# A hybrid decoder layer on one core: where the second norm's scale and shift are applied, which engine runs the first conv taps and the chain scalings, and when g2 is summed

## The chip, the cores and the metric

The kernel runs on one core of one Trainium2 chip. The metric is device time in microseconds (us); smaller is better. In the views of the profile PE is TensorE, DVE is VectorE, ACT is ScalarE, POOL is GpSimd and SP is SyncE, which issues nearly all DMAs here. PE multiplies; DVE, ACT and POOL do elementwise work; PE's results land in PSUM, from where DVE or ACT take them.

## The reference

One layer, sequence 1024, model width 1024, float32. The second half is what the change is mostly about: the norm before the MLP is `rms_norm(x, norm_mlp_w) * (1 + sc2) + sh2`.

```python
mod = silu(c) @ w_mod + b_mod                       # six vectors of 1024
sh1, sc1, g1, sh2, sc2, g2 = split(mod, 6)
h = rms_norm(x, norm_mix_w) * (1 + sc1) + sh1
proj = h @ w_in                                     # lx, ly, q, k, v, z, beta, alpha
xr = conv4(x_lru) + lru_conv_b                      # causal, 4 taps, per channel
out_lru = rms_norm(rg_lru(xr, gates) * gelu(y_lru), lru_norm_w)
q, k, v = split(silu(conv4(qkv)))                   # 4 heads of 128
out_gdn = rms_norm(gated_delta_rule(q, k, v, g, beta)) * silu(z)
x = x + g1 * (concat(out_lru, out_gdn) @ w_out)
h = rms_norm(x, norm_mlp_w) * (1 + sc2) + sh2
x = x + g2 * (square(relu(h @ w_up)) @ w_down)
return rms_norm(x, final_norm_w)
```

The gated delta rule is computed in chunks, one after the other for each head: `v_new = u - w @ state`, then the output and the next state from `v_new`.

## The kernel before

All of it is recorded first, operation by operation, and then put in order by a planner inside the kernel (`Recorder.schedule`). The large matmuls of PE are a "backbone" that keeps its written order. Everything else is placed by a list scheduler that knows a cost for each operation, a due time (how long before the backbone needs it), a bias that makes an operation less urgent (`rec.bias`), and how many buffers are free: 43 tiles of 128x1024 (`big`), later 6 more, and 8 PSUM banks. The planner's result is a fixed order for every engine; on the chip each engine runs its own list in order and waits where an operand is late. Every instruction is emitted from one line, L329, so the profile's rows are told apart by tile names and not by lines.

Almost every product is done in three matmuls: each float32 operand is split into a high part (an ACT copy to a shorter float, suffix `h`) and a low part (the remainder, a subtraction on DVE or POOL, suffix `l`), and high x high, high x low and low x high are added in PSUM (`mm3`). So each operand costs one ACT and one DVE or POOL instruction before PE can use it.

In order of time the stages are:

- **Start** (to about 65 us): x is loaded, the first modulation vectors are summed from `w_mod`, x is transposed.
- **Keys and gates** (to about 186 us): projections k0 to k3 and z0 to z3; in parallel the 64x64 triangular blocks are inverted.
- **Chains** (to about 420 us): for heads 0 to 3 the projections q and v, and `chain(h)`, 8 steps in a row. A step is: PE `ch<-S` (not in the first), DVE `r = nv - ch`, PE `ch<-r,LT`, a scaling of that PSUM piece of 128x128 by a column (`vn`, line 1018), PE `ch<-vn,ktl`, DVE `S` (the next state). The steps run between projection matmuls, which keep PE busy meanwhile.
- **LRU** (to 465 us): projections lx0..lx3 and ly0..ly3, and `lru(ct)`: a four-tap conv (`conv`, lines 813 to 819; tile `xr`), split of `xr`, gate matmuls, tanh, exp and sqrt on ACT (`ta`, `ti`, `aa`, `a`), a scan on DVE, a gelu (`tg`, `ly_st`), a store.
- **wg** (from 465 us) and **wl** (from 530 us, to 580): the output projection. wg is the half from the delta rule (rows 4 to 7 of w_out in `wo4h/wo4l` to `wo7h/wo7l`, left operands `gch/gcl`), wl the half from the LRU (`wo0` to `wo3`, `lch/lcl`). `wout(k)` scales a block of w_out on DVE by g1 and splits it; the low part is on POOL for even k, on DVE for odd k.
- **norm2(t)**: after each of the eight row tiles of wl, the second norm and its transposes (`h2T`), which are stored as raw operands `h2r`.
- **up** (580 to 899 us): a Strassen-like product for h @ w_up: 16 column pairs `up(n)`, each with seven products whose left operands are sums of pieces of h2 (`sums2`: operand numbers 1, 2, 3 are pieces alone, 6, 5, 7, 4 are sums). PE takes for pairs 0 to 3 products 1 and 2 first, then 6, 5, 7, then 4, 3.
- **down** (899 to 1209 us): the same kind of product with w_down, then the final norm.

The four modulation vectors that are needed late, g1, sc2, sh2 and g2, are made by `mod_row` (lines 931 to 954), recorded after projections z3, q1, v2 and lx0. It loads eight tiles of 512 KB, adds them scaled by silu(c) (one ACT and seven DVE instructions into `acc`), splits the sum (ACT copy, POOL subtraction), multiplies with a column of ones (four matmuls into a row of 1x1024), adds the bias, and stores the row in DRAM. `mod_bc` later loads it spread over 128 partitions. In the profile's names the tiles are `g_acc, g_h, g_l, g_r, g_b` for g1 and g2, `sc_...` and `sh_...` for sc2 and sh2 (and for the first norm's vectors at the start).

## Time and profile before

| | |
|---|---|
| median of 3 runs | 1218.96 us (1216.51 to 1219.65) |
| the profiled execution | 1220.9 us, its span 1219.1 us |
| busy: PE, DVE, ACT, POOL | 1146.6, 869.4, 579.9, 420.6 us |
| share of the span: PE, DVE, ACT, POOL | 94%, 71%, 48%, 34% |
| data moved by DMA | 230.58 MB, 189 GB/s on average |
| mean granted TensorE clock | 0.973 of full speed |

A view of the profile names an instruction by engine, operation and tiles (`out<-in`), its shape, its duration, and in square brackets how long its engine was idle before it and what released it. A busy PE is not a PE at its peak: a matmul's row is longer than its distance to the next start, so in the prediction PE's pace is read from start to start. The idle time of an engine that is not the bottleneck costs nothing by itself.

### The profile page before, as it was taken

The numbers are of one execution on the slowest core, as the hardware profiler recorded it, in microseconds if no ns is written. First come the engines' busy times: TensorE is split into PE (matmuls) and PEld (weight loads), VectorE is DVE, ScalarE is ACT, GpSimd is POOL, SyncE is SP. The second block draws the span as 40 slices with busy tenths as digits, with TensorE's granted clock in tenths as the row PEclk, the third lists the DMA queues.
The fourth block names the chain that finished last, engine by engine and source line by source line (L and its number), as shares of the span: only waits on it lengthen the run. The fifth ranks groups of instructions, "written<-read, shape, count | busy, mean of one in ns | idle before, by whom it ended". The sixth has DMA issues, their size and how long they took to land.

```text
span 1219.1 us, 15965 instructions
## 1 busy us (share of the span) xinstructions
PE 1146.6 (94%) x5912; PEld 988.9 (81%) x5912; DVE 869.4 (71%) x1150; ACT 579.9 (48%) x937; POOL 420.6 (34%) x240
## 2 busy tenths in 40 slices
...
GB/s 320 209 46 112 144 134 19 207 93 160 146 141 102 201 218 250 23 155 92 82 99 248 221 246 209 245 225 235 239 405 407 378 173 240 307 223 198 188 157 69
DMA packets 127433, 230.58 MB, mean 189 GB/s; under 512 B 10686, under 2 KB 51827, under 8 KB 127356
## 3 DMA queue, kind: packets, MB, share of 16 engines
...
q8 instruction: 46, 0.75, 0.2%
...
## 4 chain that ended last, share of the span: by engine, by line
PE 80%; DVE 9%; ACT 3%; issue 2%; DMA 2%; SPq 2%; POOL 1%; POOLq 0%; ACTq 0%; DVEq 0%
PE dn L329 25%; PE upx L329 14%; PE upz L329 7%; PE wg L329 4%; PE wl L329 4%; PE upy L329 3%; PE v_p L329 3%; PE ly_p L329 3%; PE q_p L329 3%; PE k_p L329 3%; PE lx_p L329 2%; SPq L329 2%; PE ch L329 1%; DVE xx L329 1%; DVE ftmp L329 1%
## 5 line engine op out<-in xcount | busy, mean ns | idle before, releaser
L329 PE MATMUL upx<-h2h,U 128*128 128x512 f32 x512 | 168.4, 395 | 2.5 <-DVE U L329 2.5
L329 POOL TENSOR_TENSOR wd<-wd,wd 128x512 f32<-128x512 f32 x32 | 42.8, 1343 | 232.0 <-DMA wd<-in_w_down_dram 215.2
L329 PEld LDWEIGHTS upx<-h2h,U 128*128 128x128 f32 x512 | 96.1, 188 | 25.3 <-DVE U L329 2.9
L329 PE MATMUL upx<-h2l,U 128*128 128x512 f32 x256 | 101.0, 395 | 1.2 <-DVE h2l L329 1.2
L329 ACT ACTIVATE act<-act 128x512 f32<-128x512 f32 x112 | 70.9, 633 | 61.7 <-DVE act L329 60.2
L329 DVE TENSOR_TENSOR U<-wu,U 128x512 fp32r<-128x512 f32 x112 | 81.1, 747 | 14.6 <-ACT U L329 14.5
L329 PE MATMUL upz<-h2h,U 128*128 128x512 f32 x256 | 85.2, 394 | 0.0
L329 DVE TENSOR_TENSOR act<-upz,ek 128x512 f32<-128x512 f32 x32 | 22.1, 691 | 83.0 <-PE upz L329 59.0
L329 ACT CAST U<-wu 128x512 fp32r<-128x512 f32 x112 | 65.3, 618 | 7.1 <-DVE wu L329 4.6
L329 PEld LDWEIGHTS upx<-h2l,U 128*128 128x128 f32 x256 | 48.1, 188 | 13.0 <-DVE h2l L329 1.6
L329 PEld LDWEIGHTS upz<-h2h,U 128*128 128x128 f32 x256 | 48.1, 188 | 11.3
L329 POOL TENSOR_TENSOR xb<-xb,keep 128x512 f32<-128x512 f32 x8 | 12.0, 1513 | 126.0 <-DVE keep L329 126.0
L329 ACT COPY ek<-upx 128x512 f32<-128x512 f32 x48 | 28.1, 586 | 56.7 <-PE upx L329 55.5
L329 PE MATMUL upz<-h2l,U 128*128 128x512 f32 x128 | 50.5, 394 | 1.2 <-DVE h2l L329 1.2
L329 PE MATMUL upy<-h2h,U 128*128 128x512 f32 x128 | 42.9, 394 | 0.0
L329 PE MATMUL k_p<-hh,k_wh 128*128 128x342 f32 x96 | 32.5, 338 | 6.2 <-DVE hl L329 3.5
L329 PE MATMUL z_p<-hh,z_wl 128*128 128x342 f32 x96 | 31.6, 329 | 6.0 <-POOL z_wl L329 6.0
L329 PE MATMUL lx_p<-hh,lx_wl 128*128 128x342 f32 x96 | 31.7, 330 | 1.6 <-POOL lx_wl L329 1.6
L329 DVE TENSOR_TENSOR wu<-wu,wu 128x512 f32<-128x512 f32 x48 | 33.0, 708 | 0.0
L329 PE MATMUL k_p<-hl,k_wh 128*128 128x342 f32 x96 | 32.4, 338 | 0.0
L329 PE MATMUL v_p<-hh,v_wh 128*128 128x342 f32 x96 | 32.0, 333 | 0.0
L329 PE MATMUL lx_p<-hh,lx_wh 128*128 128x342 f32 x96 | 31.9, 332 | 0.0
...
## 6 DMA issues: line engine op xcount, KB each, us to landing
...
```

The lines of the kernel that those rows point to most:

```text
L329: op.fn(*[res(v) for v in op.a], **{n: res(v) for n, v in op.k.items()})
```

## The change

Four things are changed; the computed function is the same.

1. **Second norm.** sc2 and sh2 are no longer rows spread over 128 partitions but columns [128, 8] (`mod_col`): eight 128x1 float32 matmuls of pieces of `acc` with ones, and a DVE addition. norm_mlp_w is loaded at the start with the other vectors (eight more rows in `rows2`, one more small DMA). `norm2(t)` only scales x1 by the reciprocal root (ACT, for t = 7 DVE); scale and shift are applied when the transposes leave PSUM, since there the model dimension lies on partitions: pieces of 128x128, half on DVE, half on ACT. Gone per row tile are a DVE multiplication of 128x1024, an addition of 128x1024 on POOL (for t = 7 on DVE), and four ACT copies of 128x256; pieces used alone are now split from SBUF.
2. **ScalarE.** The first tap of each of the 16 convs and the chain's `vn` (32 of them) go from DVE to ACT.
3. **g2.** It is no longer summed after projection lx0, but one eighth per pair in pairs 2 to 9 of the up phase; its row is made at pair 11.
4. **sums2.** The sums for operand 7 and operand 5 are recorded in two steps instead of one, the differences `b21` go from POOL to DVE, and products of pairs 0 and 1 (and of the last two pairs) alternate: 6(0), 6(1), 5(0), 5(1), 7(0), 7(1), where before it was 6, 5, 7 of pair 0, then of pair 1.

The diff, cut to its core:

```diff
--- before.py
+++ after.py
...
@@ -584,6 +584,7 @@
             SP.dma_start(out=rows2[48:56, :], in_=norm_mix_w.rearrange("a (r p) -> (a r) p", p=P))
+            SP.dma_start(out=rows2[56:64, :], in_=norm_mlp_w.rearrange("a (r p) -> (a r) p", p=P))
...
@@ -812,9 +813,9 @@
 
     def conv(dst, st, taps, bias=None):
         if bias is None:
-            V.tensor_scalar(dst, st[:, 0:T], taps[0], None, op0=ALU.mult)
+            A.mul(dst, st[:, 0:T], taps[0])
         else:
-            V.tensor_scalar(dst, st[:, 0:T], taps[0], bias, op0=ALU.mult, op1=ALU.add)
+            A.activation(dst, st[:, 0:T], AF.Identity, scale=taps[0], bias=bias)
         for j in range(1, 4):
             V.scalar_tensor_tensor(out=dst, in0=st[:, j:j + T], scalar=taps[j], in1=dst, op0=ALU.mult, op1=ALU.add)
 
@@ -926,20 +927,37 @@
               lambda h, s, q0, p: V.tensor_tensor(out=LT[:, q0:q0 + 4, :], in0=p, in1=xt[h][:, s, :], op=ALU.add))
 
 
-    mod_d = dp.tile([4, D], F32, tag="modd", name="modd")
-
-    def mod_row(vec, slot, name):
-        rec.bias = 40.0
+    mod_d = dp.tile([2, D], F32, tag="modd", name="modd")
+
+    def mod_part(vec, name, acc, k):
+        wt = big(f"{name}_w{k}")
+        SP.dma_start(out=wt, in_=wm_r[k, :, vec * D:(vec + 1) * D])
+        macc(acc, wt, k, k == 0)
+
+    def mod_sum(vec, name):
         acc = big(f"{name}_acc")
         for k in range(NK):
-            wt = big(f"{name}_w{k}")
-            SP.dma_start(out=wt, in_=wm_r[k, :, vec * D:(vec + 1) * D])
-            macc(acc, wt, k, k == 0)
+            mod_part(vec, name, acc, k)
+        return acc
+
+
+    def mod_col(vec, name):
+        rec.bias = 40.0
+        acc, o = mod_sum(vec, name), small(name, NK)
+        pc = ps(f"{name}_c")
+        for k in range(NK):
+            mm(pc[:, k:k + 1], acc[:, k * P:(k + 1) * P], ones[:, 0:1])
+        V.tensor_tensor(out=o, in0=pc[:, :NK], in1=bcol[:, vec * 8:vec * 8 + 8], op=ALU.add)
+        if vec == 4:
+            V.scalar_tensor_tensor(out=o, in0=o, scalar=1.0, in1=bcol[:, 56:64], op0=ALU.add, op1=ALU.mult)
+        rec.bias = 0.0
+        return o
+
+    def mod_row(vec, slot, name, acc=None):
+        rec.bias = 40.0
+        acc = acc or mod_sum(vec, name)
         row = big(f"{name}_b")[0:1, :]
         SP.dma_start(out=row, in_=b_mod[0:1, vec * D:(vec + 1) * D])
-        if vec == 4:
-            nrow = big(f"{name}_n")[0:1, :]
-            SP.dma_start(out=nrow, in_=norm_mlp_w)
         ah, al = big(f"{name}_h", F32R), big(f"{name}_l", F32R)
         A.copy(ah, acc)
         G.tensor_tensor(out=al, in0=acc, in1=ah.bitcast(F32), op=ALU.subtract)
@@ -948,8 +966,6 @@
             mm(pr_, onesr, ah[:, s], True, False)
             mm(pr_, onesr, al[:, s], False, True)
             V.tensor_tensor(out=row[:, s], in0=pr_, in1=row[:, s], op=ALU.add)
-            if vec == 4:
-                V.scalar_tensor_tensor(out=row[:, s], in0=row[:, s], scalar=1.0, in1=nrow[:, s], op0=ALU.add, op1=ALU.mult)
         SP.dma_start(out=mod_d[slot:slot + 1, :], in_=row)
         rec.bias = 0.0
 
@@ -1015,7 +1031,7 @@
                 V.tensor_tensor(out=rr, in0=nv[:, ts_], in1=pc_[:, 0:128], op=ALU.subtract)
             mm(pc_[:, 128:256], LT[:, i, :], rr)
             vn = chunk(f"vn{h}_{t}")
-            V.tensor_scalar(vn, pc_[:, 128:256], bcoef[:, i:i + 1], None, op0=ALU.mult)
+            A.mul(vn, pc_[:, 128:256], bcoef[:, i:i + 1])
             if t < NT - 1:
                 mm(pc_[:, 256:384], ktail[:, ts_], vn)
                 S2 = chunk(f"S{h}_{t}")
@@ -1146,11 +1162,9 @@
         if i == 7:
             mod_row(2, 0, "g1")
         if i == 10:
-            mod_row(4, 1, "sc2")
+            A2 = mod_col(4, "sc2")
         if i == 13:
-            mod_row(3, 2, "sh2")
-        if i == 16:
-            mod_row(5, 3, "g2")
+            sh2 = mod_col(3, "sh2")
     pl = ps("lrus")
     for t in range(NT):
         mm(pl[:, t:t + 1], msum[:, t * P:(t + 1) * P], ones[:, 0:1])
@@ -1224,9 +1237,11 @@
         A.activation(h2, x1[t], AF.Square, accum_out=ssq1[:, t:t + 1])
         V.tensor_scalar(ssq1[:, t:t + 1], ssq1[:, t:t + 1], 1.0 / D, 1e-6, op0=ALU.mult, op1=ALU.add)
         rsqrt8(ssq1[:, t:t + 1], ssq1[:, t:t + 1])
-        V.scalar_tensor_tensor(out=h2, in0=x1[t], scalar=ssq1[:, t:t + 1], in1=A2, op0=ALU.mult, op1=ALU.mult)
         SP.dma_start(out=x1_d[t], in_=x1[t])
-        (V if t == 7 else G).tensor_tensor(out=h2, in0=h2, in1=sh2, op=ALU.add)
+        if t == 7:
+            V.tensor_scalar(h2, x1[t], ssq1[:, t:t + 1], None, op0=ALU.mult)
+        else:
+            A.mul(h2, x1[t], ssq1[:, t:t + 1])
         hf, tt = t // 4, t % 4
         for g in range(2):
             ph = ps(f"h2T{t}_{g}")
...
@@ -1234,12 +1249,18 @@
                 tr(ph[:, j * P:(j + 1) * P], h2[:, (g * 4 + j) * P:(g * 4 + j + 1) * P], ident)
             for e in range(2):
                 at_ = lambda q_: v3(q_, 512)[:, :, tt * P:(tt + 1) * P]
-                pv = v3(ph[:, e * 256:(e + 1) * 256])
-                A.copy(at_(raw2[(g, hf)][e]), pv)
+                rv = at_(raw2[(g, hf)][e])
+                for j in range(2):
+                    k = 4 * g + 2 * e + j
+                    pk, sc, sh = ph[:, (2 * e + j) * P:(2 * e + j + 1) * P], A2[:, k:k + 1], sh2[:, k:k + 1]
+                    if j:
+                        A.activation(rv[:, j, :], pk, AF.Identity, scale=sc, bias=sh)
+                    else:
+                        V.tensor_scalar(rv[:, j, :], pk, sc, sh, op0=ALU.mult, op1=ALU.add)
                 if (g, hf) in alone:
                     av, bv = (at_(q_) for q_ in opb[alone[(g, hf)]][e])
-                    A.copy(av, pv)
-                    V.tensor_tensor(out=bv, in0=pv, in1=av.bitcast(F32), op=ALU.subtract)
+                    A.copy(av, rv)
+                    V.tensor_tensor(out=bv, in0=rv, in1=av.bitcast(F32), op=ALU.subtract)
 
 
     def sums2():
@@ -1261,11 +1282,12 @@
             b11, b12, b21, b22 = raws(e)
             V.tensor_tensor(out=b22, in0=b22, in1=b11, op=ALU.subtract)
         split(5, (1, 1))
+        yield
         split(7, (0, 1))
         yield
         for e in range(2):
             b11, b12, b21, b22 = raws(e)
-            G.tensor_tensor(out=b21, in0=b21, in1=b11, op=ALU.subtract)
+            V.tensor_tensor(out=b21, in0=b21, in1=b11, op=ALU.subtract)
         split(4, (1, 0))
         yield
 
@@ -1358,7 +1380,9 @@
         pz = ps(f"upz{n}")
         product(px, 6, next(w), False, True)
         A.copy(ek[:, hi_], px)
+        yield
         product(pz, 5, next(w), True, True)
+        yield
         product(px, 7, next(w), False, True)
         A.copy(ek[:, lo_], px)
         V.tensor_tensor(out=c22, in0=pz, in1=ek[:, lo_], op=ALU.add)
@@ -1383,29 +1407,39 @@
     ups = [up(n) for n in range(NP2)]
     sums = sums2()
     begun = 0
+    g2_acc = None
 
     def begin():
         nonlocal begun
         next(ups[begun])
         begun += 1
 
-    for more in (0, 0, 1, 1, 1):
-        if more:
-            next(sums)
-        if begun < 4:
-            begin()
-    for n in range(0, NP2, 2):
-        pair = range(n, n + 2)
-        if n in (0, NP2 - 2):
-            for at in range(2):
-                for m in pair:
-                    next(ups[m])
-        else:
+    def both(pair, steps):
+        for at in range(steps):
             for m in pair:
                 next(ups[m])
-                begin()
-                next(ups[m])
-                sums_down(m - 2)
+            yield
+
+    begin()
+    begin()
+    next(sums)
+    begin()
+    begin()
+    for _ in both(range(2), 4):
+        next(sums, None)
+    for m in range(2, NP2 - 2):
+        for at in range(3):
+            next(ups[m])
+        begin()
+        next(ups[m])
+        sums_down(m - 2)
+        if m < 10:
+            g2_acc = g2_acc or big("g2_acc")
+            mod_part(5, "g2", g2_acc, m - 2)
+        if m == 11:
+            mod_row(5, 1, "g2", g2_acc)
+    for _ in both(range(NP2 - 2, NP2), 4):
+        pass
     for m in range(NP2 - 4, NP2):
         sums_down(m)
 
...
```

How the planner's order moves at three places (names as in the stages above; the number at a name's end is that of the recorded tile):

VectorE where wg begins, before. `xr_4247`, `ta_4353` and `ly_st` are lru(2), `xr_4507` is lru(3); the scalings `wo<-wo,gnwh,g_bc` and `wo5l`, `wo7l` make wg's operands.

```order
L329 SCALAR_TENSOR_TENSOR wo_4198<-wo_4198,gnwh,g_bc 128x1024
L329 TENSOR_SCALAR ta_4353<-ta_4353 128x1024
L329 SCALAR_TENSOR_TENSOR wo_4201<-wo_4201,gnwh,g_bc 128x1024
L329 TENSOR_TENSOR xr_4247<-xr_4247,ta_4353 128x1024
L329 COPY ly_b<-ly_p_4273 128x1
L329 SCALAR_TENSOR_TENSOR xr_4247<-aa_4376,xr_4247 128x1024
L329 TENSOR_TENSOR wo5l<-wo_4198,wo5h 128x1024
L329 TENSOR_TENSOR ly_st<-ly_st,xr_4247 128x1024
L329 TENSOR_TENSOR wo7l<-wo_4201,wo7h 128x1024
L329 TENSOR_SCALAR xr_4507<-lx_st,cols 128x1024
```

VectorE there with the change (`xr_4122`, `ta_4347` are lru(2), `xr_4434` is lru(3)):

```order
L329 SCALAR_TENSOR_TENSOR ly_st<-tg_4182,ly_st 128x1024
L329 SCALAR_TENSOR_TENSOR wo_3934<-wo_3934,gnwh,g_bc 128x1024
L329 SCALAR_TENSOR_TENSOR wo_3937<-wo_3937,gnwh,g_bc 128x1024
L329 COPY ly_b<-ly_p_4263 128x1
L329 TENSOR_TENSOR wo5l<-wo_3934,wo5h 128x1024
L329 SCALAR_TENSOR_TENSOR xr_4122<-ti_4361,xr_4122 128x1024
L329 SCALAR_TENSOR_TENSOR ta_4347<-a_4423,ta_4347 128x1024
L329 TENSOR_TENSOR wo7l<-wo_3937,wo7h 128x1024
L329 TENSOR_SCALAR ta_4347<-ta_4347 128x1024
L329 SCALAR_TENSOR_TENSOR xr_4434<-lx_st,cols,xr_4434 128x1024
L329 SCALAR_TENSOR_TENSOR tg_4438<-tg_4438,ly_st 128x1024
L329 TENSOR_TENSOR xr_4122<-xr_4122,ta_4347 128x1024
```

`wo5l` stood behind the product and the scan of lru(2); it now stands ahead of lru(2)'s remaining operations (from `xr<-ti` on), behind the last projection's column copy `ly_b`. The additions into `g_acc`, which stood some rows further up, are gone from this stage.

GpSimd at the same place, before and then with the change (`gcl` are left operands of wg, `xrl` is lru(2)'s, `g_l` the low part of g2's sum):

```order
L329 TENSOR_TENSOR ly_wl<-ly_w,ly_wh 128x1024
L329 TENSOR_TENSOR msum<-msum,lsq_4179 128x1024
L329 TENSOR_TENSOR gcl_4322<-gcm_4203,gch_4296 128x512
L329 TENSOR_TENSOR xrl_4343<-xr_4247,xrh_4328 128x1024
L329 TENSOR_TENSOR gcl_4322<-gcm_4271,gch_4296 128x512
L329 TENSOR_TENSOR g_l<-g_acc,g_h 128x1024
L329 TENSOR_TENSOR wo4l<-wo_4166,wo4h 128x1024
```

```order
L329 TENSOR_TENSOR ly_wl<-ly_w,ly_wh 128x1024
L329 TENSOR_TENSOR wo4l<-wo_3898,wo4h 128x1024
L329 TENSOR_TENSOR msum<-msum,lsq_4192 128x1024
L329 TENSOR_TENSOR gcl_4256<-gcm_4054,gch_4160 128x512
L329 TENSOR_TENSOR gcl_4256<-gcm_4057,gch_4160 128x512
L329 TENSOR_TENSOR xrl_4302<-xr_4122,xrh_4269 128x1024
L329 TENSOR_TENSOR wo6l<-wo_3924,wo6h 128x1024
```

`wo4l` follows the last split of a projection's weights directly; before, five other operations stood between. `wo6l` now stands behind `xrl`.

The chain of head 0: VectorE before (`vn`, `r` and `S` are chain steps), and ScalarE with the change:

```order
L329 TENSOR_TENSOR r_4_2501<-nv_2288,ch_4_2492 128x128
L329 TENSOR_SCALAR v1T<-v_st,cols 128x1024
L329 TENSOR_SCALAR vn_4_2533<-ch_4_2492,bcoef 128x128
L329 SCALAR_TENSOR_TENSOR v1T<-v_st,cols,v1T 128x1024
L329 SCALAR_TENSOR_TENSOR S_4_2559<-S_3_2483,egl,ch_4_2492 128x128
L329 TENSOR_TENSOR g_b<-g_r_2519,g_b 1x512
L329 TENSOR_TENSOR g_b<-g_r_2521,g_b 1x512
L329 TENSOR_TENSOR r_5_2578<-nv_2288,ch_5_2570 128x128
```

```order
L329 ACTIVATE zt_2505<-zz_2472 128x1024
L329 CAST g_h<-g_acc 128x1024
L329 ACTIVATE vn_4_2528<-ch_4_2488,bcoef 128x128
L329 CAST v_wh<-v_w 128x1024
L329 ACTIVATE vn_5_2591<-ch_5_2573,bcoef 128x128
L329 ACTIVATE v1th<-v1T 128x1024
L329 ACTIVATE q_st<-q_p_2475,q_b 128x340
```

`vn` leaves VectorE, where it stood between operations of 128x1024, and stands on ScalarE between a cast of `g_acc`, a cast of projection weights `v_wh` and a tanh of 128x1024.

11 lines of the change are left out of this document (5 added, 6 removed).

## The prediction

> **What bounds the kernel now.** The page first: PE is busy 94% of the span and holds 80% of the chain that ended last, so only two things can shorten it: less PE work, or less time in which PE waits. I therefore read PE's waits, summed by what released them (us in total, times, longest), since each is a place where a faster neighbour is worth something.
>
> ```profile
> PE wg L329 <- DVE wo5l L329: 7.2, 1, 7.2
> ...
> PE wg L329 <- POOL wo4l L329: 5.2, 1, 5.2
> ...
> PE ch L329 <- DVE vn L329: 3.3, 3, 1.4
> ...
> PE upx L329 <- DVE U L329: 2.5, 1, 2.5
> PE sc_r L329 <- POOL sc_l L329: 2.4, 1, 2.4
> ...
> PE lx_p L329 <- POOL lx_wl L329: 1.6, 1, 1.6
> ...
> PE upz L329 <- DVE h2l L329: 1.2, 1, 1.2
> PE upx L329 <- DVE h2l L329: 1.2, 1, 1.2
> ...
> PE ch L329 <- DVE lx_st L329: 0.9, 1, 0.9
> PE ch L329 <- DVE r L329: 0.9, 1, 0.9
> ```
>
> What is left out lies at the start and in the key stage, which the change barely touches, or is below 0.9. The rows fall into three places: the chains (vn, sc_l, lx_wl, lx_st, r: 9.1), the start of wg (7.2 + 5.2) and the sums ahead of the up phase (2.5 + 1.2 + 1.2). Next the same stretches by engine (us; busy time and count of PE, its weight loads, DVE, ACT, POOL; granted clock, DMA share, GB/s).
>
> ```profile
> 240.00:420.00 180.00, 169.62 (x1151) 163.24 (x1150) 157.35 (x222) 74.48 (x109) 65.10 (x24) 0.99 0.42 139
> 465.11:485.36 20.25, 7.84 (x18) 5.49 (x18) 17.38 (x12) 11.99 (x15) 16.26 (x5) 0.58 0.57 226
> 600.00:618.00 18.00, 13.15 (x55) 9.73 (x54) 18.00 (x17) 10.47 (x15) 3.73 (x2) 1.00 0.08 29
> 618.00:900.00 282.00, 282.00 (x1217) 228.29 (x1216) 170.86 (x260) 154.16 (x265) 60.86 (x46) 1.00 0.68 234
> ```
>
> In the chains DVE is busy 87% (157.35 of 180) and ACT 41%; at wg and at the sums DVE is full while PE stands. In the up phase PE never waits, and DVE has 39% free. So DVE limits exactly the places from which this change takes work.
>
> **Start of wg.** PE's timeline, then DVE's and POOL's:
>
> ```profile
> 465.11 0.50 PE L329 MATMUL wg<-wo4h,gch 128*128 128x512 f32 x1 [0.56 <-ACT wo4h L329]
> 470.81 0.80 PE L329 MATMUL wg<-wo4l,gch 128*128 128x512 f32 x1 [5.20 <-POOL wo4l L329]
> ...
> 479.66 0.80 PE L329 MATMUL wg<-wo5l,gch 128*128 128x512 f32 x1 [7.21 <-DVE wo5l L329]
> ...
> 485.36 0.40 PE L329 MATMUL wg<-wo5h,gcl 128*128 128x512 f32 x1
> 485.60 0.40 PE L329 MATMUL wg<-wo6h,gch 128*128 128x512 f32 x1
> ```
> ```profile
> 451.90 3.44 DVE L329 SCALAR_TENSOR_TENSOR g_acc<-g_w,cact,g_acc 128x1024 f32<-128x1024 f32 x1
> ...
> 471.42 2.78 DVE L329 TENSOR_TENSOR xr<-xr,ta 128x1024 f32<-128x1024 f32 x1 [2.87 <-ACT ta L329]
> ...
> 474.23 3.24 DVE L329 TENSOR_TENSOR_SCAN xr<-aa,xr 128x1024 f32<-128x1024 f32 x1
> 477.40 2.21 DVE L329 TENSOR_TENSOR wo5l<-wo,wo5h 128x1024 fp32r<-128x1024 f32 x1
> ```
> ```profile
> 456.56 3.25 POOL L329 TENSOR_TENSOR g_l<-g_acc,g_h 128x1024 fp32r<-128x1024 f32 x1
> 465.13 5.62 POOL L329 TENSOR_TENSOR wo4l<-wo,wo4h 128x1024 fp32r<-128x1024 f32 x1 [5.32 <-ACT wo4h L329]
> ```
>
> wo5l itself takes 2.21 us, but it stands in DVE's list behind a wait of 2.87 for lru(2)'s square root, its product and its scan. g2's additions, one of 3.44 us among them, had pushed all of that to the end of the projections. With g2 gone, the new order puts wo4l right behind the last projection split on POOL and wo5l ahead of lru(2)'s tail. The three waits make 0.56 + 5.20 + 7.21 = 13.0. Then PE is slow for a while: 18 matmuls start between 465.11 and 485.36, 20.25 us; without the 12.4 us of the two waits after the first, 7.85. At the pace right behind (485.36 to 485.60, about 0.23 as most starts there) they need 4.1, so the slow pace costs 3.7. In all 16.7 us stand here. I leave 2 for the first operands (wo6l is behind xrl on POOL) and look at what is late next, wl's left operand from lru(3):
>
> ```profile
> 516.22 1.66 DVE L329 TENSOR_TENSOR ly_st<-ly_st,xr 128x1024 f32<-128x1024 f32 x1
> ...
> 527.50 1.30 POOL L329 TENSOR_TENSOR lcl<-lcm,lch 128x512 fp32r<-128x512 f32 x1
> 530.40 0.39 PE L329 MATMUL wl<-wo0h,lch 128*128 128x512 f32 x1
> ```
>
> That path (ly_st, store, load, split) ends at 528.8, and wl's tenth matmul uses it at about 530.4 + 9 x 0.23 = 532.5: a margin of 3.7. wg moves up by some 14 us, but lru(3) does too, since it follows lru(2), whose tail no longer waits behind g2's additions and whose first tap is on ACT; I take it to move by 12, which leaves the margin at 1.7, and set 2 aside for it. Term: **-13** (bounds -6, if only one of the two waits goes, and -16.7).
>
> **Chains.** What leaves DVE or goes to ACT, and the nearest rows for its price there:
>
> ```profile
> L329 DVE TENSOR_SCALAR vn<-ch,bcoef 128x128 f32<-128x128 f32 x32 | 10.9, 347 | 4.9 <-PE ch L329 4.4
> ...
> L329 DVE TENSOR_SCALAR v1T<-v_st,cols 128x1024 f32<-128x1024 f32 x1 | 2.5, 2453 | 0.0
> ...
> L329 DVE TENSOR_SCALAR v3T<-v_st,cols 128x1024 f32<-128x1024 f32 x1 | 0.7, 746 | 0.0
> ...
> L329 ACT ACTIVATE q_dm<-q_dm,ngc 128x128 f32<-128x128 f32 x32 | 10.0, 392 | 3.3 <-POOL q_dm L329 3.3
> ...
> L329 ACT ACTIVATE g_acc<-g_w,cact 128x1024 f32<-128x1024 f32 x2 | 2.3, 1146 | 0.0
> ```
>
> DVE loses 10.9 for vn and, between 240 and 420, about ten first taps of 0.75 to 2.45, say 12: 157 becomes 134 of 180. ACT gains 32 x 0.39 + 10 x 1.15 = 24: 74 becomes 98, 54%. Certain is the 2.4 of sc_r <- sc_l: that low part and the row matmuls no longer exist. Likely is lx_wl's 1.6, as POOL also drops two splits, each like the g_l above (3.25). The 5.1 of vn, lx_st and r came from vn and r queuing behind DVE operations of 128x1024; r has fewer of them now, but vn queues behind ACT's. I count 1 of the 5.1. Against it stands that a vn on ACT is 0.045 longer (392 to 347): on the 28 links of the four chains 1.3. Term: **-5 + 1.3** (bounds -9 and +8: 28 links x 0.3, the mean rest of a 1.1 us operation ahead at 54% load).
>
> VectorE against ScalarE is where a rule speaks against this change. The Trainium skill, "ScalarE: Activation LUTs" (section "Rules for kernel authors"), says to do multiplications and additions on VectorE, not ScalarE. The rows agree on the single operation (0.75 against 1.15 for an undisturbed tap). By that rule alone the moves lose 10 x 0.40 + 32 x 0.045 = 5 us of engine time. But "Perfetto Trace Analysis" ("Optimizing Scalar/DVE Operations") of the skill allows moving work to ScalarE when VectorE is saturated, and 87% here is near that; so I hold with the second, and the first feeds the rival on the slow side.
>
> **Sums.** The change gives PE 24 more matmuls of pair 0 and 1 (6 of both, then 5 of both) before each later operand is used, and takes the b21 differences off POOL, where they disturbed DVE:
>
> ```profile
> 602.72 3.31 POOL L329 TENSOR_TENSOR h2r<-h2r,h2r 128x1024 f32<-128x1024 f32 x1 [2.30 <-DVE h2r L329]
> 603.76 3.36 DVE L329 TENSOR_TENSOR h2l<-h2r,h2h 128x1024 fp32r<-128x1024 f32 x1
> 607.04 1.21 DVE L329 TENSOR_TENSOR h2r<-h2r,h2r 128x1024 f32<-128x1024 f32 x1
> ```
>
> An h2l beside POOL took 3.36; undisturbed 1.2. Two of them beside POOL lost 4.3, and a product pair now covers 24 x 0.23 = 5.5 for the two h2l and b22 that follow. The waits of 2.5, 1.2 and 1.2 all go: **-4.9** (bounds -2.4 and -5.5). DVE's 128-wide evictions add little: per row tile it drops a multiplication of 128x1024 (1.2, as the rows above), and ACT drops four copies.
>
> **The rest.** Columns for sc2 and sh2: eight such matmuls with ones are these (two passes each),
>
> ```profile
> 523.76 1.84 PE L329 MATMUL lrus<-ones,msum 128*128 128x1 f32 x16
> ```
>
> so +3.7 for sixteen; eight row matmuls of 512 go, 8 x 0.23: net **+1.8**. The extra small DMA ahead of the first weights: **+0.3** (0 to 1). g2 in the up phase: seven additions of 1.3 and one ACT pass, in 282 us with 111 free on DVE, and 4 MB beside a DMA share of 0.68: 0, hidden under PE; without that cover 10. Key stage: first taps of k on ACT, row order a little changed: 0 (-3 to +3).
>
> Sum: -13 - 5 + 1.3 - 4.9 + 1.8 + 0.3 = -19.5. The profiled span of 1219.1 becomes 1199.6; that execution took 1220.9 and the median of the runs is 1218.96, so I set the same 19.5 off the median: **1199.5 us**.
>
> **Rivals.**
>
> *B, wl takes back what wg gives.* lru(3)'s tail needs ta's table load, two ACT passes, a scan and a trip through DRAM; if it moves by only 4 us instead of 12, wl waits about 14 - 3.7 - 4 = 6 more, less the 2 set aside: 1204. If wo4l or wo5l also stays late, -6 instead of -13: 1207. For it: the tail's own DVE and ACT operations are unchanged. Against: its conv begins earlier.
>
> *C, the stalls move rather than go.* Only the sums and the 2.4 of sc_l are real, wg keeps its two waits by another operand: -4.9 - 2.4 + 2.1 = -5, so 1214.
>
> *D, slower: the chain is paced by ACT's list.* One mechanism: ACT keeps its order, so a vn stands until everything ahead of it has its operands. An example of such a stand:
>
> ```profile
> 455.37 1.05 ACT L329 CAST g_h<-g_acc 128x1024 fp32r<-128x1024 f32 x1 [2.21 <-DVE g_acc L329]
> ```
>
> In the new order a g_h cast stands right ahead of head 0's fifth vn. If each of the 28 links gets one full operation of 1.15 more that PE cannot fill, the chains lose 32 instead of gaining 3.7: 1218.96 - 15.8 + 32 = 1235. It decides from 15.8 / 28 = 0.56 a link on. Against: only 3 of the vn cost PE anything before, so most links have cover. The Trainium skill's rule on VectorE, above, points this way.
>
> **How the numbers follow.** A 0.57, B 0.24, C 0.10, D 0.09. A's own range is 1191 to 1206. The range for 8 in 10 reaches into B and part of C: 1190 to 1212. A difference within 0.3% (3.7 us) is what the measurement cannot tell from none: A and B are faster, C, at 5 us, for 0.06 of its 0.10; D is slower but for 0.01. So faster 0.87, same 0.05, slower 0.08.
>
> **What would show it.** Right: PE waits on wo4l and wo5l under 2 us in all and a granted clock near 1 in the first 20 us of wg; no wait of upx or upz on h2l or U; vn's rows on ACT near 0.39 and ch <- vn under 4 us in total; no PE wait between 620 and 900. Wrong: PE idle before the first or tenth wl matmul (B), a new wait of wg on wo6l or gcl (C), ch <- ACT vn of 10 us or more (D), or upx <- U in the up phase, which would mean that g2's loads delay the weights.

## The result and the profile after

The changed kernel takes 1189.03 us (median of 4 runs, 1186.78 to 1190.0) against 1218.96 (1216.51 to 1219.65): a ratio of 0.9755, 95% interval 0.9736 to 0.9775. It is faster by 29.9 us where 19.5 were forecast. The stages of the profiled executions compare as follows. The lengths are read from the traces, from the first start on PE of one kind of matmul to the first of the next:

| stage | before | after | difference | forecast |
|---|---|---|---|---|
| start, to the first modulation column (`sh_c`) | 62.9 | 59.8 | -3.1 | +0.3 |
| to the first z projection | 41.2 | 41.1 | -0.1 | 0 |
| key stage: z to the first q projection | 63.6 | 60.3 | -3.3 | 0 |
| q to the first chain step (`ch`) | 72.9 | 73.3 | +0.4 | 0 |
| chains, to the first lx projection | 90.1 | 85.1 | -5.0 | -3.7 + 1.8 |
| LRU projections, to the first `wg` | 134.3 | 128.6 | -5.7 | (in the row above) |
| wg, to the first `wl` | 65.3 | 50.8 | -14.5 | -13 |
| wl, to the first `upx` | 49.7 | 53.8 | +4.1 | 0 |
| up, to the first `dn` | 319.2 | 314.3 | -4.9 | -4.9 |
| down, to the end | 319.7 | 320.1 | +0.4 | 0 |

The first row is mostly a matter of the single execution: among the kernels below whose start is written as before, it goes from 60.1 to 62.9, among those with the new start from 59.4 to 61.8. The rows from the key stage on are not, and the experiments take them apart. Chains, LRU and wg together fall by 25.2 (289.7 to 264.5), wl pays 4.1.

PE's waits in the changed kernel (what released it; us in total, times, longest):

```profile
PE sc_c L329 <- DVE sc_acc L329: 4.6, 1, 4.6
...
PE z_p L329 <- POOL z_wl L329: 3.2, 1, 3.2
...
PE h2T L329 <- DVE h2r L329: 1.5, 3, 0.5
...
PE wg L329 <- DVE wo7l L329: 0.9, 1, 0.9
...
PE ch L329 <- ACT vn L329: 0.9, 2, 0.5
PE ch L329 <- DVE r L329: 0.9, 1, 0.9
```

The waits on wo4l (5.2) and wo5l (7.2) are gone, and so are sc_r, upx and upz; wg has 0.9 left. `sc_c` belongs to the first norm at the start. New are `h2T <- h2r`, three times 0.5, in wl. By engine in three stretches: from the first chain step to the end of `wo7l`, the first 20 us of wg, and the up phase:

```profile
234.50:451.50 217.00, 213.02 (x1440) 208.67 (x1438) 187.71 (x206) 121.70 (x187) 92.50 (x34) 0.98 0.45 149
448.20:468.20 20.00, 18.99 (x80) 14.47 (x80) 18.59 (x16) 16.90 (x22) 3.41 (x1) 1.00 0.69 269
583.00:867.00 284.00, 284.00 (x1226) 229.47 (x1225) 184.62 (x273) 157.68 (x268) 64.15 (x47) 1.00 0.74 247
```

The same first stretch before:

```profile
240.60:481.90 241.30, 217.10 (x1421) 206.38 (x1420) 214.68 (x263) 112.07 (x158) 103.60 (x37) 0.96 0.48 164
```

PE was busy 217.10 of 241.30 and is now busy 213.02 of 217.00: it has almost nothing left to wait for. VectorE gave up 26.97 us of busy time (214.68 to 187.71), and the stretch became 24.30 shorter. At wg PE starts 80 matmuls in 20 us at a granted clock of 1.00, where before it started 18 at 0.58. In the up phase PE is full although g2's additions now lie there (DVE 184.62 of 284).

PE at the start of wg, then DVE (start, duration, and in brackets the idle time and what ended it):

```profile
448.19 0.39 PE L329 MATMUL wg<-wo4h,gch 128*128 128x512 f32 x1
...
451.60 0.50 PE L329 MATMUL wg<-wo7l,gch 128*128 128x512 f32 x1 [0.93 <-DVE wo7l L329]
```
```profile
437.42 6.75 DVE L329 SCALAR_TENSOR_TENSOR wo<-wo,gnwh,g_bc 128x1024 f32<-128x1024 f32 x2
...
444.37 2.04 DVE L329 TENSOR_TENSOR wo5l<-wo,wo5h 128x1024 fp32r<-128x1024 f32 x1
...
450.32 1.22 DVE L329 TENSOR_TENSOR wo7l<-wo,wo7h 128x1024 fp32r<-128x1024 f32 x1
```

`wo5l` is done at 446.4, before wg begins at 448.19. The 32 `vn`, now on ACT, as a group (count, busy time, mean ns, idle time before them):

```profile
L329 ACT ACTIVATE vn<-ch,bcoef 128x128 f32<-128x128 f32 x32 | 11.6, 367 | 57.0 <-PE ch L329 57.0
```

A `vn` takes 0.367 on ACT against 0.347 on DVE, and ACT spends 57.0 us idle in front of its 32 `vn`, waiting for PE.

### The profile page after: what moved, and what is told of

It reads as the page before. It is cut to its first block, busy times and chain, and to the rows that moved or that the text cites. A ratio compares the mean times of both kernels' runs of the same rounds, so it can differ in the third digit from the quotient of the medians.

```text
span 1187.2 us, 15989 instructions
## 1 busy us (share of the span) xinstructions
PE 1142.0 (96%) x5936; PEld 989.2 (83%) x5936; DVE 857.9 (72%) x1125; ACT 617.3 (52%) x990; POOL 385.8 (32%) x229
## 4 chain that ended last, share of the span: by engine, by line
PE 84%; DVE 7%; issue 3%; ACT 2%; POOL 1%; DMA 1%; SPq 1%; POOLq 0%; DVEq 0%; ACTq 0%
PE dn L329 26%; PE upx L329 15%; PE upz L329 7%; PE k_p L329 4%; PE wg L329 4%; PE upy L329 4%; PE lx_p L329 3%; PE v_p L329 3%; PE ly_p L329 3%; PE wl L329 3%; PE q_p L329 2%; PE ch L329 2%; DVE xx L329 1%; DVE ftmp L329 1%; DMA x<-in_x_dram 1%
## 5 line engine op out<-in xcount | busy, mean ns | idle before, releaser
L329 DVE TENSOR_TENSOR U<-wu,U 128x512 fp32r<-128x512 f32 x112 | 76.7, 704 | 16.6 <-ACT U L329 16.5
L329 DVE TENSOR_TENSOR act<-upz,ek 128x512 f32<-128x512 f32 x32 | 22.1, 691 | 60.3 <-PE upz L329 44.9
L329 ACT COPY ek<-upx 128x512 f32<-128x512 f32 x48 | 28.1, 586 | 59.7 <-PE upx L329 59.5
L329 ACT ACTIVATE vn<-ch,bcoef 128x128 f32<-128x128 f32 x32 | 11.6, 367 | 57.0 <-PE ch L329 57.0
L329 POOL TENSOR_TENSOR ssq<-ssq,mhalf 128x1 f32<-128x1 f32 x16 | 11.7, 732 | 90.0 <-DVE ssq L329 89.9
L329 PE MATMUL k_p<-hh,k_wh 128*128 128x342 f32 x96 | 32.3, 337 | 5.0 <-DVE hl L329 3.9
L329 PE MATMUL k_p<-hh,k_wl 128*128 128x342 f32 x96 | 32.2, 335 | 0.0
```

Source lines behind the costliest of these rows:

```text
L329: op.fn(*[res(v) for v in op.a], **{n: res(v) for n, v in op.k.items()})
```

## The experiments

Two theories are held against each other in what follows; the second took this form only when the single parts did not add up, and the expectations, written before each run, use the names that they give themselves. **Local**: each of PE's waits has its own cause, so each part of the change pays where it removes a wait, and the parts add up. **Backlog**: from the first chain step to wg VectorE is behind, PE's waits are only where that shows, and the stretch follows VectorE's list.

### The parts one by one

Each kernel is the one before with a single part of the change; the computed function stays.

```diff
only_conv (in conv, both branches)
-            V.tensor_scalar(dst, st[:, 0:T], taps[0], None, op0=ALU.mult)
+            A.mul(dst, st[:, 0:T], taps[0])
only_vn
-            V.tensor_scalar(vn, pc_[:, 128:256], bcoef[:, i:i + 1], None, op0=ALU.mult)
+            A.mul(vn, pc_[:, 128:256], bcoef[:, i:i + 1])
only_g2
-        if i == 16:
-            mod_row(5, 3, "g2")
+                if m < 10:
+                    g2_acc = g2_acc or big("g2_acc")
+                    mod_part(5, "g2", g2_acc, m - 2)
+                if m == 11:
+                    mod_row(5, 3, "g2", g2_acc)
only_norm2 (rows2, mod_col and norm2 as in the change)
-            mod_row(4, 1, "sc2")
+            A2 = mod_col(4, "sc2")
only_sums (sums2, up and the loop over the pairs as in the change)
-            G.tensor_tensor(out=b21, in0=b21, in1=b11, op=ALU.subtract)
+            V.tensor_tensor(out=b21, in0=b21, in1=b11, op=ALU.subtract)
```

> The kernel before with one edit: the first tap of all 16 convs on ACT. The theory on record (the first taps are a small relief of DVE and the key stage is unchanged): 0 to -3 us, first z_p matmul within 1 us of 104.1. Rival (the unforecast 6.6 us of the start and key stage and most of the chains' extra gain come from the taps): -8 us or more, z_p first at 101 or earlier, first q_p at 162. Second rival (the planner's new order as a whole is what pays, no single edit): any sign, below 4 us.

> The kernel before with one edit: the chain's 32 scalings vn on ACT. The theory on record: -1 us won, 1.3 lost, so 0 (-2 to +2), key stage unchanged. Rival (vn on DVE was what held the chains up, and the 10.7 us that the chains and the LRU stage gave come from it): -5 us or more between the first ch and the first wg matmul. Rival D of the prediction (paced by ACT's list): slower by 5 us or more.

> The kernel before with one edit: g2 summed in pairs 2 to 9 of the up phase, its row made at pair 11. The theory on record: nearly all of wg's gain, -10 to -13 us, comes from here: the waits of wg on wo4l and wo5l go from 12.4 to under 4. Rival (g2 was only one of several things in front of wo4l and wo5l; it needs the taps and the other POOL splits gone too): -3 to -7 us, one of the two waits stays.

> The kernel before with one edit: scale and shift of the second norm as columns, applied at the eviction of the transposes. The theory on record: -4 in the chains (no sc_l, lx_wl not delayed), +1.8 of PE work, +0.3 at the start, so -2; in the wl stage 0. Rival (the eight evictions per row tile make PE wait in the wl stage, which lasted 53.9 us with the whole change and 49.7 before): -2 in the chains and +4 in wl, so +2 to +4.

> The kernel before with one edit: sums2 in smaller steps, b21 on DVE, products of pairs 0 and 1 alternating. The theory on record: -4.9 (-2.4 to -5.5), no wait of upx or upz on h2l or U between 600 and 620. Rival (the h2l are only moved: the waits stay at a later product): 0 to -2.

| kernel | median us | ratio, interval | key | chains | LRU | wg | wl | up |
|---|---|---|---|---|---|---|---|---|
| before | 1218.96 | | 63.6 | 90.1 | 134.3 | 65.3 | 49.7 | 319.2 |
| only_conv | 1214.91 | 0.9966 (0.9954 to 0.9979) | 60.4 | 88.2 | 133.8 | 67.3 | 49.7 | 318.9 |
| only_vn | 1226.94 | 1.0067 (1.0050 to 1.0084) | 63.7 | 86.0 | 142.9 | 64.8 | 48.8 | 323.8 |
| only_g2 | 1205.91 | 0.9897 (0.9882 to 0.9912) | 63.4 | 90.1 | 131.2 | 54.5 | 50.0 | 319.7 |
| only_norm2 | 1218.42 | 1.0002 (0.9993 to 1.0012) | 64.1 | 90.6 | 131.3 | 62.0 | 53.8 | 321.3 |
| only_sums | 1211.63 | 0.9942 (0.9921 to 0.9963) | 63.4 | 90.1 | 134.3 | 65.2 | 49.8 | 313.6 |

Against the runs of the kernel before beside them (1218.77, for only_sums 1219.06) the five make -3.9, +8.2, -12.9, -0.4 and -7.4, in sum -16. The change as a whole makes -29.9: the parts do not add up, and Local falls in that form.

`vn` on ACT, which was thought to be nearly free, costs 8.2 us by itself. The chain stage does become 4 shorter, but the LRU stage 8.6 longer. The waits of DVE, before and in only_vn (in the whole span):

```profile
DVE vn L329 <- PE ch L329: 4.4, 8, 1.8
DVE S L329 <- PE ch L329: 3.5, 5, 1.3
```
```profile
DVE S L329 <- PE ch L329: 12.2, 12, 2.6
```

DVE no longer waits for `vn`'s input, but it comes to `S` earlier, and `S` needs the matmul that needs `vn`. It stands 12.2 us there, against 3.5 + 4.4. The windows from the first chain step to the end of `wo7l` for only_vn, only_g2, only_norm2 and only_conv:

```profile
240.20:485.40 245.20, 220.92 (x1420) 209.74 (x1420) 213.57 (x231) 122.43 (x190) 99.06 (x37) 0.94 0.48 162
```
```profile
239.30:467.30 228.00, 213.69 (x1418) 205.31 (x1416) 199.19 (x252) 108.31 (x154) 96.92 (x36) 0.99 0.45 150
```
```profile
238.30:472.60 234.30, 215.42 (x1442) 207.97 (x1441) 201.99 (x256) 105.16 (x148) 95.66 (x35) 0.98 0.50 169
```
```profile
236.00:476.30 240.30, 214.12 (x1416) 206.63 (x1415) 205.81 (x254) 122.04 (x166) 104.80 (x38) 0.96 0.49 166
```

Subtract DVE's busy time from the length: it is idle 26.6 us before, 31.6 in only_vn, 28.8 in only_g2, 32.3 in only_norm2, 34.5 in only_conv and 29.3 in the changed kernel. Taking g2's additions away shortens its busy time by 15.5 and the stretch by 13.3. Taking the first taps away alone shortens its busy time by 8.9, of which 7.9 comes back as waiting. In only_vn even the busy time hardly falls (1.1 for 32 `vn` of together 10.9), because other operations run longer: the 14 additions into `g_acc` took 23.2 us before and 26.3 here, the four `wo<-wo,gnwh,g_bc` 7.1 and 10.2:

```profile
L329 DVE SCALAR_TENSOR_TENSOR g_acc<-g_w,cact,g_acc 128x1024 f32<-128x1024 f32 x14 | 23.2, 1658 | 0.0
...
L329 DVE SCALAR_TENSOR_TENSOR wo<-wo,gnwh,g_bc 128x1024 f32<-128x1024 f32 x4 | 7.1, 1780 | 0.0
```
```profile
L329 DVE SCALAR_TENSOR_TENSOR g_acc<-g_w,cact,g_acc 128x1024 f32<-128x1024 f32 x14 | 26.3, 1876 | 0.0
...
L329 DVE SCALAR_TENSOR_TENSOR wo<-wo,gnwh,g_bc 128x1024 f32<-128x1024 f32 x4 | 10.2, 2560 | 0.0
```

What they ran beside was not taken apart. Of only_vn's loss 4.0 us stand between the first chain step and wl; the 4.6 in the up phase (323.8 against 319.2), where nothing was changed, are open.

only_norm2 gains 5.8 on the way from the first chain step to wl (chains +0.5, LRU -3.0, wg -3.3) and gives it back in wl (+4.1) and up (+2.1). Only the sums behave as a part of their own: -5.6 in the up phase, nothing elsewhere but in the start, which varies by itself.

### The parts undone one by one

Each is the changed kernel with one part as before; again the function stays.

```diff
without_vn
-            A.mul(vn, pc_[:, 128:256], bcoef[:, i:i + 1])
+            V.tensor_scalar(vn, pc_[:, 128:256], bcoef[:, i:i + 1], None, op0=ALU.mult)
without_conv (both branches)
-            A.mul(dst, st[:, 0:T], taps[0])
+            V.tensor_scalar(dst, st[:, 0:T], taps[0], None, op0=ALU.mult)
without_g2
+        if i == 16:
+            mod_row(5, 1, "g2")
-            mod_part(5, "g2", g2_acc, m - 2)
without_norm2
-            A2 = mod_col(4, "sc2")
+            mod_row(4, 1, "sc2")
```

> The changed kernel with one edit undone: vn back on DVE. Alone, vn on ACT cost 8.4 us. If edits add up, this kernel is faster than the changed one by about 8 (1181). Rival (vn on ACT was dear only beside g2's additions and casts; with g2, sc2's and sh2's casts gone from ACT and POOL it costs nothing): within 3 us of 1189. Second rival (with the other edits made it is vn that gives the chains' extra gain): slower, 1193 or more, the stretch from the first ch to the first wg matmul longer than 214 us (213.7 in the changed kernel, 224.4 before).

> The changed kernel with one edit undone: g2 summed after lx0 again. Alone, g2 gave 12.9. If edits add up: 1202. If wg's gain needs g2 and the others together (the singles sum to about -14 with the sums still to be measured, the whole is -30): more than that is lost, 1207 or above, with waits of wg on wo4l or wo5l back over 5 us. If the others have made g2's move superfluous: under 1195.

> The changed kernel with one edit undone: second norm as before (rows, DVE and POOL passes over 128x1024). Alone it gave 0: 8 us faster up to the first wl matmul, 4 lost in wl, 2 in the sums. If edits add up: 1189 (within 2). If its gain ahead of wl lasts only when the sums are also changed: 1193 to 1197. In both cases the wl stage (first wl to first upx matmul) is back from 53.9 to about 50 us.

> The changed kernel with one edit undone: first taps back on DVE. All four kernels with the taps on ACT took 60.3 to 60.4 us from the first z_p to the first q_p matmul, all without 63.4 to 64.1: here 63.5. If that is all: 1192 to 1193. If the taps also shape the order at wg as the other edits do: 1197 or more with a wait of wg over 4 us.

| kernel | median us | ratio to before, interval | key | chains | LRU | wg | wl | up |
|---|---|---|---|---|---|---|---|---|
| after | 1189.03 | 0.9755 (0.9736 to 0.9775) | 60.3 | 85.1 | 128.6 | 50.8 | 53.8 | 314.3 |
| without_vn | 1194.47 | 0.9788 (0.9768 to 0.9809) | 60.4 | 86.4 | 128.1 | 56.7 | 53.7 | 313.7 |
| without_g2 | 1199.57 | 0.9835 (0.9821 to 0.9850) | 60.3 | 85.0 | 130.9 | 61.4 | 52.5 | 313.8 |
| without_norm2 | 1198.19 | 0.9826 (0.9809 to 0.9842) | 60.4 | 85.1 | 128.9 | 62.4 | 49.7 | 314.5 |
| without_conv | 1198.89 | 0.9830 (0.9814 to 0.9846) | 63.9 | 87.0 | 130.0 | 55.4 | 53.9 | 314.4 |

Undone, the four cost 5.4, 10.5, 9.2 and 9.9 us. `vn` on ACT loses 8.2 when it is alone and seems to gain about 5 beside the others (the intervals of the two ratios overlap); norm2 gains nothing alone and 9 beside them. For `vn`, g2 and norm2 nearly all of the loss stands at wg (+5.9, +10.6, +11.6), and of the taps' loss 4.6, beside 3.6 in the key stage. Chains and LRU together stay in all four within 3.3 us of the changed kernel's 213.7, so the delay shows at the end of the stretch, as Backlog has it. But more work on DVE is not what these traces show everywhere. From the first chain step to the end of `wo7l`, without_vn and then without_conv:

```profile
234.90:457.00 222.10, 213.74 (x1440) 208.17 (x1438) 182.99 (x240) 117.12 (x160) 89.94 (x34) 0.98 0.45 153
```
```profile
236.60:459.70 223.10, 214.02 (x1441) 207.53 (x1440) 184.30 (x215) 114.41 (x181) 90.30 (x34) 0.99 0.46 152
```

With `vn` or the taps back on DVE, DVE is busy for less than the 187.71 of the changed kernel, and idle for 39.1 and 38.8 instead of 29.3. In these two the stretch grew by waits inside DVE's list, in the order that the planner gave it. For g2 and norm2 its busy time did grow, by 8.5 and 3.9 (196.17 and 191.59).

### Is it where `wo5l` stands in the list?

without_norm2 brings the wait at wg back, larger than before. Its PE waits, and DVE ahead of `wo5l`:

```profile
PE wg L329 <- DVE wo5l L329: 10.8, 1, 10.8
```
```profile
457.44 1.56 DVE L329 TENSOR_TENSOR xr<-xr,ta 128x1024 f32<-128x1024 f32 x1 [1.73 <-ACT ta L329]
...
459.04 2.29 DVE L329 TENSOR_TENSOR_SCAN xr<-aa,xr 128x1024 f32<-128x1024 f32 x1
...
461.25 1.20 DVE L329 TENSOR_TENSOR wo5l<-wo,wo5h 128x1024 fp32r<-128x1024 f32 x1
```

Here `wo5l` is behind lru(2)'s product and scan again, as in the kernel before. This is the third theory, **position**: the gain is that the planner happened to put `wo5l` ahead of the scan. If so, it must be had by ordering alone. Two kernels, on before and on without_norm2, make wg's operands more urgent:

```diff
+    rec.bias = -10.0
     gw_ = [wout(k) for k in range(4, 8)]
+    rec.bias = 0.0
```

> The kernel before, with no work changed: the four scalings and splits of wg's weights only get a due time 10 us earlier. wo5l then stands ahead of lru(2)'s product and scan in DVE's list, wo4l stays behind the same operations on POOL. If the place in the list is what made wg wait on wo5l: that wait falls from 7.2 to under 3 and 3 to 6 us are won (1213 to 1216), the wait on wo4l stays near 5. If DVE is simply full there (capacity, not place): the wait only moves to wo7l, gcl or wl's operands, within 2 us of before.

> The changed kernel with norm2 undone (1198.2; wg waits 10.8 us for wo5l, which stands behind lru(2)'s product and scan there) and the same earlier due time for wg's weights, which puts wo5l ahead of them; no work is changed against the run without norm2. If the place of wo5l in DVE's list is all that norm2 gave at wg: the 10.8 goes to under 3, wg takes under 55 us instead of 62.4, 1188 to 1192. If norm2's smaller DVE and POOL load was needed: the wait moves, 1196 or more.

wo_early: 1219.22 us, ratio 1.0003 (0.9992 to 1.0015). without_norm2_wo_early: 1203.18 us, 0.9861 (0.9837 to 0.9884), 5 slower than without_norm2; its wg is as long (62.8 against 62.4), and the loss stands in the up phase (320.5 against 314.5). The wait on `wo5l` went in both, and this came instead (wo_early, then without_norm2_wo_early):

```profile
PE wg L329 <- POOL wo4l L329: 4.1, 1, 4.1
...
PE wg L329 <- DVE wo7l L329: 2.5, 1, 2.5
```
```profile
PE wg L329 <- POOL gcl L329: 6.8, 3, 3.8
```

Position falls: `wo5l` ahead of the scan is not enough. The stage from wg to wl is 65.0 in wo_early against 65.3. With about the same work in the lists, another operand is the last. Whether some other order of the same work would do better is open.

### Which engine limits: extra work on PE, extra work on DVE

The pads are work with no use: on PE, 72 matmuls of 342 columns in the projections lx0, ly0, lx1, ly1, whose result the next ones overwrite (72 x 0.157 = 11.3 us); on DVE, 16 additions of 128x512 that nothing reads (16 x 0.69 = 11 us). Both were put into the kernel before and into the changed one.

```diff
pe_pad_before, pe_pad_after (in Proj.third)
+            for n in range(6 if self.name in ("lx0", "ly0", "lx1", "ly1") else 0):
+                mm(p[:, 0:342], self.w[0][:, 0:P], hT[0][0][:, s])
dve_pad_before, dve_pad_after (behind those projections)
+            for n in range(4):
+                V.tensor_tensor(out=pad, in0=q_.dst[:, 0:512], in1=q_.dst[:, 512:1024], op=ALU.add)
```

> The kernel before with 72 more matmuls of 342 columns on PE (6 in each third of the projections lx0, ly0, lx1, ly1; their result is overwritten by the real group): 72 x 0.157 = 11.3 us of PE work that depends on nothing new. In all kernels so far the first wl matmul came 48.3 us (47.5 to 49.2) after DVE had finished the last low part of wg's weights. If that end of DVE's list is what limits the stretch from the first chain to wg, PE has 17.7 us there to spare: the kernel gets 0 to 4 us slower, and the waits of wg fall from 12.4 to about 3. If PE's own work limits it (as the separate terms of the prediction assume, each PE wait a loss by itself): 11 us slower.

> The kernel before with 16 more DVE additions of 128x512 on the staged outputs of lx0, ly0, lx1, ly1 (result unused): 16 x 0.69 = 11 us. If the end of DVE's list limits: 9 to 13 us slower, the last of wo5l, wo7l ends about 11 later (481.9 before), and the first wl matmul follows 48 us behind it. If there is slack in DVE (it was idle for 26.6 of the 241 us between the first ch matmul and wo7l): under 5.

> The changed kernel with the same 72 matmuls on PE. There wo7l ends 3.5 us after PE's last projection matmul instead of 17.7, and wg waits only about 1: PE is nearly the limit itself. 8 to 11 us slower than the changed kernel (1197 to 1200). If DVE still limits as before: under 4 (1193).

> The changed kernel with the same 16 DVE additions as in dve_pad_before (11 us). 11.3 us more on PE cost the changed kernel 6.9 (1195.9), so PE has become the larger part of the limit there, but wo7l still ends 3.5 us after PE's last projection. If DVE limits together with PE: 6 to 11 us slower than 1189 (1195 to 1200). If the change has given DVE room: under 4 (1193).

| kernel | median us | ratio to before, interval | LRU | wg |
|---|---|---|---|---|
| pe_pad_before | 1220.72 | 1.0018 (1.0008 to 1.0029) | 141.3 | 57.9 |
| dve_pad_before | 1229.55 | 1.0089 (1.0067 to 1.0110) | 142.4 | 67.4 |
| pe_pad_after | 1195.93 | 0.9806 (0.9789 to 0.9822) | 137.7 | 49.1 |
| dve_pad_after | 1198.91 | 0.9835 (0.9819 to 0.9850) | 129.2 | 60.1 |

In the kernel before, 11.3 us more for PE cost 1.5 us against the runs beside it (1219.24; by the ratio 2.2). PE arrives later at wg and waits less there:

```profile
PE wg L329 <- DVE wo5l L329: 5.0, 1, 5.0
```

The stretch from the first chain step to the end of `wo7l` is as long as without the pad, 241.20 against 241.30; the first wl follows 48.5 us after that end in both. First pe_pad_before, then dve_pad_before:

```profile
236.60:477.80 241.20, 227.71 (x1493) 218.67 (x1491) 208.20 (x260) 111.08 (x156) 102.33 (x37) 0.98 0.45 152
```
```profile
237.40:487.80 250.40, 223.42 (x1419) 211.32 (x1418) 212.30 (x275) 109.39 (x154) 103.74 (x37) 0.93 0.46 158
```

The same amount on DVE cost 10.3 us and made the stretch 9.1 longer. So in the kernel before PE does not limit this stretch; that is shown. For DVE the proof is less clean, as its second row tells: its busy time did not rise (212.30, against 214.68), because other operations were shorter (beside the pads some 200 us in sum); the added length is in waits of its list, the longest of 8.1 put down to POOL:

```profile
DVE xr L329 <- POOL wo6l L329: 8.1, 1, 8.1
```

What limits is thus, as far as these runs go, DVE's list with everything it waits for, in its order. Its busy time alone is not the measure. No pad was put on ACT or POOL, so how much of the length their lists set is open.

In the changed kernel the PE pad costs 6.9 and the DVE pad 9.9: now both matter. In dve_pad_after the wait at wg is back:

```profile
PE wg L329 <- DVE wo5l L329: 6.0, 1, 6.0
```

### The key stage

The forecast gave it 0. k_taps_only moves the first tap to ACT in the four key convs alone, on the kernel before:

```diff
-        conv(y, st, [col("gcw", j * 12 + ct) for j in range(4)])
+        conv(y, st, [col("gcw", j * 12 + ct) for j in range(4)], act=name[0] == "k")
```

> The kernel before with only the four key convs' first taps on ACT. If the key stage's 3.3 us come from those taps (the wait of z_p on z_wl was 6.0 without them and 3.2 with them): z_p to q_p 60.4, wait 3.2, and nothing else: 1215 to 1216. If the q, v and lru taps matter for it: 63.5 and 1218 to 1219.

1215.29 us, 0.9966 (0.9951 to 0.9982): the same ratio as all 16 taps in only_conv. The key stage is 60.4 instead of 63.6, and PE's wait there is the one of the changed kernel, 3.2, where the kernel before has 6.0. Before, then k_taps_only:

```profile
PE z_p L329 <- POOL z_wl L329: 6.0, 1, 6.0
```
```profile
PE z_p L329 <- POOL z_wl L329: 3.2, 1, 3.2
```

So alone only the key taps pay; the other twelve seem to pay when the rest of the list is shorter too (without_conv loses 4.6 at wg).

### The new cost in wl

wl became 4.1 longer, and norm2 is its cause (only_norm2 53.8, without_norm2 49.7). 0.9 of it is work: 56 transposes of `h` fall into it instead of 48, by the order. PE in the changed kernel, then DVE at the same place:

```profile
537.94 0.49 PE L329 MATMUL h2T<-ident,h 128*128 128x128 f32 x3
538.93 0.76 PE L329 MATMUL h2T<-ident,h 128*128 128x128 f32 x5 [0.50 <-DVE h2r L329]
```
```profile
538.47 0.41 DVE L329 TENSOR_SCALAR h2r<-h2T,sc,sh 128x128 f32<-128x128 f32 x1 [0.50 <-PE h2T L329]
```

The planner has put the eviction of the first piece between the third and the fourth transpose into the same PSUM bank, and the fourth waits until that eviction is done. wlfix makes each eviction depend on the last of the four transposes (the first line stands behind these, the others behind each eviction); wlfix_z1 adds to it that one low part of z's weights, behind which PE stands 3.2 at the z projections, goes from POOL to DVE.

```diff
wlfix
+            last = len(rec.ops) - 1
+                    if last not in rec.ops[-1].preds:
+                        rec.ops[-1].preds[last] = 1
+                        rec.ops[last].succs.append(len(rec.ops) - 1)
wlfix_z1, further
-            G.tensor_tensor(out=self.w[1], in0=raw, in1=self.w[0].bitcast(F32), op=ALU.subtract)
+            (V if self.name == "z1" else G).tensor_tensor(out=self.w[1], in0=raw, in1=self.w[0].bitcast(F32), op=ALU.subtract)
```

> The changed kernel with one dependency added in the planner: the evictions of h2T's pieces are placed behind all four transposes of their bank. In the changed kernel PE waits 0.5 between the third and the fourth transpose in rows, released by DVE's eviction of the bank's first piece, and the wl stage lasts 53.8 us instead of 49.7 (0.9 of it for 8 transposes that stood later before). If that order is the cause: wl stage 51 or under, 2 to 3 us won (1186 to 1187). If the evictions are simply too slow for PE: no change, the waits only move to the first transpose of the next bank.

> wlfix (1184.7) with one more edit: the low part of projection z1's weights is made on DVE instead of POOL. PE waited 3.2 us for it behind POOL's pow and fills. If POOL's queue is the cause: z_p to q_p falls from 60.4 to 58 or less, 1182 to 1183. If the end of DVE's list or the block inverse behind it decides: no gain, the wait on xn (4.1) grows by as much.

wlfix: 1184.73 us (1183.29 to 1186.13), 0.9718 (0.9703 to 0.9732), faster than both kernels. Of the 4.3 us gained, 2.1 stand in wl (51.7 instead of 53.8) and 1.0 in the up phase (313.3 instead of 314.3); the rest lies in the profiles ahead of the key stage and in the down phase, where the kernels are alike, and is put down to nothing here. The eight transposes of a row tile now run without a break:

```profile
535.79 1.07 PE L329 MATMUL h2T<-ident,h 128*128 128x128 f32 x8
536.62 0.48 PE L329 MATMUL wl<-wo1l,lch 128*128 128x512 f32 x1
```

wlfix_z1 lost: 1194.05 us, 0.9791 (0.9768 to 0.9815). The wait it aimed at fell from 3.2 to 0.4, but the key stage became longer (61.7 against 60.4 in wlfix), and so did wg (59.5 against 50.8), where nothing had been touched. PE stands there for DVE's addition `x<-wg,x`, which empties a PSUM bank:

```profile
PE wg L329 <- DVE x L329: 6.7, 1, 6.7
...
PE z_p L329 <- DVE z_wl L329: 0.4, 1, 0.4
```

The moved subtraction takes 1.2 us on DVE and the kernel lost 9.3, so the work itself is not the reason: with that one operation the planner's order changed far behind it (`wo7l` ends 3.1 us ahead of the last projection, in wlfix 3.2 behind it). In without_norm2_wo_early, too, 5 us came from order alone. So the 5 to 10 us that a part costs when undone are not its price; a shift of the order is mixed into them.

## Why the prediction was right or wrong

**What bounds the kernel: half right.** "DVE limits exactly the places from which this change takes work" holds, and the views read for it were the right ones. The conclusion drawn from it was wrong.

**The step that failed** is the one that turns PE's waits into a sum: "The rows fall into three places", and each place was priced by its own waits, the chains at 5 of their 9.1 (2.4, 1.6 and "1 of the 5.1"). From the first chain step to wl the terms make -14.9 (-5 + 1.3 + 1.8 - 13). Measured are -25.2, and these 10.3 are nearly the whole miss of 10.4. The key stage (-3.3) and wl (+4.1), both put at 0, were missed too and nearly cancel each other; that is luck.

What the runs show in its place: between the first chain step and wl the waits are not separate losses. The PE pad shows it: 11.3 us more work ahead of wg cost about 2, as PE then waited less at wg. A wait removed early would likewise be expected to reappear at wg while the lists that PE waits for stay as long. With the whole change nearly all the rows went together: PE's waits from the first chain step to wg from 11.1 to 3.1 us, those at the start of wg from 13.0 to 0.9. The listed waits were not even all of the loss: of 224.4 us between the first chain step and wg PE's matmuls need 205.5 (each shape's count by its median distance from start to start), which leaves 18.9, twice the 9.1 of the rows (the rest are shorter waits and a slower pace). In the changed kernel 7.8 of 213.7 are left.

That VectorE's list set this length is what the pads and g2 speak for; it is not shown as cleanly. With the whole change DVE's busy time fell by 27.0 us and the stretch to the end of `wo7l` by 24.3. The number that came nearest stood in the prediction, "157 becomes 134 of 180": 23 us of relief, g2's additions not counted. It is a bound and not a price: only_conv relieves DVE by 8.9 and makes the stretch 0.9 shorter.

**wg, -13: right** in size (-14.5) and in what would show it (0.9 left, clock 1.00). The reason given, that `wo4l` and `wo5l` change places, is not the cause by itself: with `wo5l` early alone the time stays (wo_early), and without norm2, which has nothing to do with these operands, the wait is back at 10.8. What remains, as an argument and not a measurement, is that less stood ahead of them.

**Chains, -5 + 1.3: under-sized**; chains and LRU stage give -10.7 with the columns' matmuls in them. The price of `vn` on ACT was fine (0.367 measured, 0.39 taken). That "I count 1 of the 5.1" was too little, since `ch <- vn` fell from 3.3 to 0.9. The Trainium skill's "ScalarE: Activation LUTs" ("Rules for kernel authors") keeps multiplications on VectorE, and "Perfetto Trace Analysis" ("Optimizing Scalar/DVE Operations") lets them go when it is saturated. The runs of `vn` decide for neither: with VectorE busy 214.68 of 241.30 us the move alone lost 8.2 us, and in the changed kernel it seems to bring about 5. The longer operation itself (0.367 against 0.347) makes only 32 x 0.020 = 0.6 of the loss.

**Sums, -4.9: right.** -4.9 in the changed kernel, -5.6 alone, and no wait of upx or upz on h2l or U is left in it.

**Columns +1.8: right** as work: 32 matmuls of 128x1, 0.112 apart, make 3.6 in place of eight of 128x512, 0.236 apart, which made 1.9. **Start +0.3** is within what the start varies by. **g2 in the up phase, 0: right**; PE has no wait there.

**Key stage, 0 (-3 to +3): wrong by 3.3**, just outside its bounds. The four key taps on ACT take 2.8 off the wait for z's weights.

**wl: not in the sum.** Set aside were 2 for wl's left operand; that never came late. Of the 4.1, 0.9 are the eight transposes more and 2.1 the evictions between transposes, which wlfix takes away and at which the prediction did not look; 1.1 is left open.

So the measured terms are -3.3 (key), -25.2 (first chain step to wl), +4.1 (wl) and -4.9 (up), together -29.3, against -29.9 in the medians.

**Rivals.** B did not come: no wait of wl on its left operands. C, that the stalls move, is what wo_early does, but not the change. D's sign is true of `vn` alone, by another mechanism: `vn` does not queue behind ACT's list (57.0 us of idle time before it); DVE waits at `S` for the longer way round.
